# The weights of 32 experts, regrouped by the host: one row of 16 KB or 8 KB for each partition in place of rows of 2 KB and 4 KB

## The chip, the core and the metric

The kernel runs on one core of one Trainium2 chip. The metric is the device time of one execution in microseconds. Before the change three runs took 2957.39 to 2959.16 us, with a median of 2958.98 us.

## What the kernel computes

All of it is one launch in 32-bit floats, on 512 tokens of 1024 channels. A first block (rmsnorm, sparse attention beside a linear recurrence, a dense feed-forward, a gated embedding) takes the first half of the time and is not touched by the change. A second block has two layers. Each modulates its input by a vector, mixes tokens by windowed attention and local mixers, projects by `w_out`, normalizes, and then passes the tokens through a hierarchical mixture of experts. Layer 0 sends 768 tokens there (512 and 256 of a context), layer 1 only the 512. Cut to what matters here:

```python
# hier_moe(h, ...): h is [n, 1024]; 4 groups of 8 experts, top 1 group, top 2 experts in it
g_val, g_idx = lax.top_k(hf @ w_rg + b_rg, 1)
e_val, e_idx = lax.top_k(e_logit_of_the_group, 2)
gates  = p_group[:, None] * jax.nn.softmax(e_val, axis=-1)
expert = g_idx * 8 + e_idx
...
# for each block of tokens that go to one expert e; w1, w3: [32, 1024, 512], w2: [32, 512, 1024]
y = (jax.nn.silu(xb @ w1[e]) * (xb @ w3[e])) @ w2[e]
...
return jnp.zeros_like(h).at[slot_tok].add(ys * slot_gate[:, None])
```

An expert's weights are 2.10 MB for each of w1, w3 and w2. With 32 experts a layer's weights are 201 MB, and on-chip memory holds those of three experts at a time.

## The kernel before

The expert stage of a layer is the function `experts(l)` (L1788 to L1953). Its tokens have been sorted by expert into *items* of 64 slots in layer 0 and of 32 slots in layer 1; each item belongs to one expert. The static part of the program handles 41 items in layer 0 and 51 in layer 1, and a loop at its end takes what may be left over. Which expert an item has is known only at run time: SP, the engine that issues the weight loads, reads the number `eid` and a flag `new` from memory into registers.

For one item the work is this. POOL gathers the tokens' rows with an indirect DMA (L1813), some items ahead. PE transposes them (L1819, ACT copies them out at L1821), then multiplies by w1 and w3 in two halves (`first`, L1832; the result is the tile `ph`). `silu` is a tanh on ACT (L1838) and two steps on DVE (L1839, L1840). PE transposes again, then multiplies by w2 in two halves (`second`, L1847, tile `py`). `scatter` scales the result by the gate on DVE (L1859; in layer 0 a step at L1858 first prepares the tile `ys`), and POOL writes it to DRAM with an indirect DMA (L1860). The tile `ys` has three buffers in layer 0, and L1858 is the first to write one again. The program's order on PE is fixed by hand: an item's second product runs behind the first product of the next item.

**Places for weights.** There are three. Each holds two tiles of 16 KB per partition for w1 and w3 (`R13`, shape 128 x 4 x 2 x 512: in each of four row blocks the row of w1, then that of w3) and two tiles of 8 KB per partition for w2 (`R2`, 128 x 2 x 1024). Even items use place 0, odd items places 1 and 2 by turns:

```python
def place(i):
    return 0 if i % 2 == 0 else 1 + i // 2 % 2
...
ld(i + (4 if i % 2 else 2), n)     # behind each product group n of item i
```

`ld(i, n)` (L1881 to L1888) asks for piece n of item i: pieces 0 and 1 are halves of w1 and w3, 2 and 3 halves of w2. It is called behind the product group that used that piece of the place last, so two items ahead for even items and four ahead for odd ones. The load carries the condition `new > 0`: where the place already holds that expert, the DMA is skipped, but its instruction remains. Even items run through the experts with the most items, so long runs of them load nothing; odd items mostly take a new expert each.

**The load itself** is `expert_load` (L1770 to L1786). Pieces 0 and 1 are two DMAs of 1 MB each, one from w1 and one from w3, whose rows are 512 floats or 2 KB. Pieces 2 and 3 are one DMA of 1 MB each with rows of 1024 floats or 4 KB. An item has six loads. In the trace they are all written `r<-w`, on SP's queue, L1786, or L1782 for those without a condition.

**What else is on the queue.** Three experts are chosen ahead, and their weights are loaded without a condition before the routing is known: `load_front` (L1726) for place 0, `open_second` and `open_third` for place 1, `open_fourth` and `expert_store` for place 2. Around them `wload` (L159 to L165) loads other weights in rows of 1 KB, among them the chunks of `w_out`, that ACT (L156) and DVE (L157) split into two parts for PE. At the end `moe_norm` (L1959) reads the tile `yd` back in rows of 8 KB. SP issues one DMA after the other; each has one of eight completion semaphores, DMAHW0 to DMAHW7 by turns, and an instruction that reuses one waits until the DMA that had it before has landed. What the text doesn't pin in order (`pin`) is placed by the scheduler of the framework that builds the program.

Of the kernel before, what the change touches and what calls it, by code (L numbers as in the profile page):

```python
# [32 lines left out]
def constants():  # L33
    c = {}
# [19 lines left out]
    # for the routing: 0.., order of experts, 8.., 256 (token tile - 128), offsets of the parts of rows, 2 p, p;  # L54
    # the work block of an item: a + total * b - places of the second lane * c
# [14 lines left out]
class Stream:  # L70
    """Column chunks of weights [1024, 256 each], split into (hi, lo) by halves of their rows, a half
    ahead of the products; the last ones are only loaded. The chunks asked for count from a base."""
# [33 lines left out]
class Kern:  # L106
# [16 lines left out]
    def rsqrt(self, pool, v, scale, eps):  # L123
        """1/sqrt(v*scale+eps) for a [128, 1] tile: a bit guess and three Newton steps, each on a
        multiple c of the root (c becomes -2 c^3), divided out in the end."""
# [21 lines left out]
    def mm3(self, out, stat, mov, start, stop):  # L147
        """out += stat.T @ mov with each side a (hi, lo) pair."""
        nc = self.nc
        (sh, sl), (mh, ml) = stat, mov  # L150
        nc.tensor.matmul(out, sh, mh, start=start, stop=False)  # L151
        nc.tensor.matmul(out, sh, ml, start=False, stop=False)  # L152
        nc.tensor.matmul(out, sl, mh, start=False, stop=stop)  # L153
# [13 lines left out]
    def wchunk(self, ap, kt, cols, pool=None, raw=None):  # L167
        """A [kt*128, cols] piece of a weight as a list of kt (hi, lo) pairs [128, cols]."""
# [68 lines left out]
    def vectors(self, z, engine):  # L237
        """Per-channel vectors with the channel on the partition."""
# [15 lines left out]
    def norm_hT(self, pool, x, gain, hi, lo, work):  # L254
        """rmsnorm of x [128, 4, 1024] (token, channel), transposed to (hi, lo) [128, 8, 512]."""
# [39 lines left out]
    def proj(self, w, N=512):  # L295
        """The two 128-channel tiles of a 256-column chunk as [channel, token] in PSUM."""
# [10 lines left out]
    def projg(self, W, c, N):  # L307
        """The same from a stream, in steps."""
# [12 lines left out]
    def fill(self):  # L321
        """One step of work that is not tied to the place where it runs."""
        if self.bg is not None:
            next(self.bg, None)
# [11 lines left out]
    def mixer(self):  # L336
        nc, tc, a = self.nc, self.tc, self.a
        with ExitStack() as st:
# [21 lines left out]
            # gates: 0.5 * sigmoid, [token, tile, 48]  # L360
# [45 lines left out]
    def keys(self, m):  # L406
        """Keys of groups 2m, 2m+1 with (hi, hi) and (lo, lo) stacked."""
# [16 lines left out]
    def compress(self, kp):  # L424
        """Compressed keys (hi, hi / lo, lo stacked) and values (two copies of the 32 rows)."""
# [57 lines left out]
    def gelu2(self, out, x, pool, shape, tag):  # L483
        """2 * gelu(x) (tanh form); x in SBUF."""
# [7 lines left out]
    def pair(self, t, Q, KD):  # L492
        """Heads 2t and 2t+1: half the gated sum of the three branches, [channel, token]."""
# [4 lines left out]
        # compressed branch  # L498
# [34 lines left out]
        # the two dense branches  # L533
# [43 lines left out]
    def rnn_vectors(self):  # L577
# [11 lines left out]
        # softplus(-lam) = max(-lam, 0) + log1p(exp(-|lam|)), exp as ((1+t)/(1-t))^16 with t = tanh(-|lam|/32)  # L589
# [9 lines left out]
        # log1p(e) = 2 atanh(z), z = e / (2 + e) <= 1/3  # L599
# [21 lines left out]
    def rnn(self, c, yA):  # L621
        """Channels 256c..: conv, RG-LRU and the mixing gates; the sum with yA to y (hi, lo)."""
# [22 lines left out]
        for m in range(2):  # L645
# [9 lines left out]
            # y = (1 + exp(log_a)) / 2 is about 1/(1-th), th = tanh(log_a / 2), and one Newton step makes it so  # L655
# [5 lines left out]
            # a = (1+th)/(1-th), sqrt(1-a^2) = 2 sqrt(-th)/(1-th)  # L661
# [23 lines left out]
    def row(self, pool, name, ap, n=D, engine=None):  # L685
        """A vector on all partitions."""
        t = pool.tile([128, n], F32, name=self.nm(name), tag=name)
        (engine or self.nc.scalar).dma_start(t, bass.AP(tensor=ap.tensor, offset=ap.offset, ap=[[0, 128], [1, n]]))
        return t

    def mix_out(self, xb):
        """x + rmsnorm(y @ w_out)."""
# [17 lines left out]
    def norm_add(self, x, o, g, pool):  # L710
        """x += rmsnorm(o) * g for one token tile."""
# [66 lines left out]
    def ple(self):  # L778
        """x + sigmoid(x @ w_gate + b) * (p @ w_proj), by [channel, token]; leaves x and its transpose."""
# [48 lines left out]
    def modulation(self, pool, pp, pt_pool):  # L828
        """silu(c) @ w_ada + b_ada for both conditionings, a step at a time: by rows in DRAM
        (modd) and by channel on the partition (modT)."""  # L830
# [58 lines left out]
    def mcol(self, l, r, n):  # L889
        """Modulation vector n of layer l and conditioning r, channel on the partition: [128, 8]."""  # L890
        return self.modT[l][:, r, 8 * n:8 * n + 8]

    def mrow(self, pool, l, r, n, tag, engine=None):
        """The same on all partitions: [128, 1024]."""
# [11 lines left out]
    def transposeN(self, src, n, j, tag="pp"):  # L906
        """Channel tile j of n token tiles, transposed into PSUM: [128, n * 128]."""
# [5 lines left out]
    def affine_split(self, hi, lo, src, sc, sh, pool):  # L913
        """(hi, lo) of src * sc + sh with per-partition scalars."""
# [81 lines left out]
    def open_route(self, l, NT, pool, kv):  # L996
        """What the routing keeps of each token tile, and the routers' biases."""
# [14 lines left out]
    def logit_parts(self, l, r, wg, c12):  # L1012
        """For the logits of (t scale + shift) gs + bs, which are scale (t @ wg) + shift c1 + c2."""
# [24 lines left out]
    def open_side(self, l, r):  # L1038
        """Tokens of the sequence (r = 0) or of the context (r = 1)."""
# [15 lines left out]
    def side_input(self, c):  # L1055
        """The modulated input, transposed, as (hi, lo); in the second layer with stops after the norms."""
# [40 lines left out]
    def stream(self, l):  # L1097
        """The chunks of w_in_2 and w_out_2 in the order of their use."""
# [3 lines left out]
    def tokpairs(self, W, c, NT):  # L1102
        """[token, 256] products, two token tiles to a PSUM bank."""
# [8 lines left out]
    def rope(self, out, src, i, nh, wk):  # L1112
        """Axial rotary embedding of token tile i: src [128, nh * 64] in PSUM."""
# [12 lines left out]
    def project(self, c):  # L1126
        """Keys, values and queries, attention and the local mixers: c.mix."""
# [82 lines left out]
    def attention(self, Q, NT, r, mix, wk, sp, op_):  # L1210
        """All heads: window and context keys (sequence) or context keys only. The scores run ahead of
        the transposes of the weights."""
# [5 lines left out]
        for u in range(len(units) + LAG):  # L1218
# [10 lines left out]
            if nl:  # L1229
# [3 lines left out]
                # key block m, queries of block n at slot n - m + 1  # L1233
# [27 lines left out]
    def scores(self, h, n, q, NT, r, wk, sp):  # L1261
        """The softmax of one head and query block: [query, window keys and context keys]."""
# [87 lines left out]
    def layer_norm(self, x, src, pool):  # L1350
        """x = (src - mean) / sqrt(var + eps) over the channels of one token tile."""
# [7 lines left out]
    def ln_scale(self, st, pool):  # L1359
        """(scale, shift) that normalize a token tile."""  # L1360
# [8 lines left out]
    def side_out(self, c, po, steps=None):  # L1369
        """o @ w_out, first layer norm, the expert input (to DRAM) and the router's logits, whose  # L1370
        products run behind; steps: of other work, to go between."""
# [71 lines left out]
        def logits(t, h, w):  # L1443
            """Of half the channels of a token tile, in two steps."""
# [73 lines left out]
    def pick(self, i0, i1, le, pool):  # L1518
        """The group and, in each group, the first and second expert of token tiles i0 .. i1 as one-hot
        rows; the first of equals is taken."""  # L1520
# [42 lines left out]
    def route(self, l, NT, ep):  # L1563
        """Experts, gates and the list of work: blocks of slots, each of one expert. The experts are
        ordered by their number of blocks; the first and the last are given."""
# [13 lines left out]
        with ExitStack() as st:  # L1579
# [13 lines left out]
            # blocks of the experts, [all, expert] and on the partition, and where they begin  # L1593
# [22 lines left out]
            # slots  # L1616
# [9 lines left out]
            # the place of work block d, u = total - 1 - d: 2 d, or else, of each two odd places the first for  # L1626
            # 0 <= u <= nb and the second for others; u = 1 has place 3
# [8 lines left out]
            # rows of a slot, in ng parts: ng times its token, less an offset where it is in use, and the choice  # L1636
# [19 lines left out]
            # items: expert of each, and how many  # L1656
# [19 lines left out]
            # odd items have two places  # L1676
# [6 lines left out]
            # gates  # L1683
# [29 lines left out]
    def given(self, s):  # L1713
        """The expert whose weights are in place s before the routing."""
        return slice(STATIC[s], STATIC[s] + 1)

    def open_front(self, l):
        """Places for the weights of the experts: some are there before the routing, for experts that are
        given their items."""
# [20 lines left out]
    def place16(self, name, *shape, dt=F32):  # L1740
        """One of four places of 16 KB: for a chunk of w_out, then for an expert's weights."""
# [28 lines left out]
    def expert_load(self, l, s, n, e, cond=None, engine=None, pin=None):  # L1770
        """Pieces 0, 1: half the rows of w1 and w3; 2, 3: half the rows of w2; to place s."""
        nc, a = self.nc, self.a
        pick = lambda w, r: a[w][l][e, r, :]
        if n < 2:
            r = slice(n * 512, (n + 1) * 512)
            prs = [(self.R13[s][n][:, :, z, :], pick(w, r)) for z, w in enumerate(("w1_2", "w3_2"))]
        else:
            prs = [(self.R2[s][n - 2], pick("w2_2", slice((n - 2) * 256, (n - 1) * 256)))]
        for dst, src in prs:
            src = src.rearrange("o (k p) c -> p (o k) c", p=128)  # L1780
            if cond is None:
                d = (engine or nc.sync).dma_start(dst, src)  # L1782
                if pin:
                    pin(d)
            else:
                nc.sync.dma_start(dst, src, cond=cond, bounds_check="skip_entire_dma")  # L1786

    def experts(self, l, NT, ep):  # L1788
        """Items of some slots, one expert each. Even items take the experts from the front of the list,
# [211 lines left out]
```

## Time and profile before

| | |
|---|---|
| time, median of three runs | 2958.98 us |
| span of the profiled execution | 2959.7 us |
| PE (matmul) busy | 2529.7 us, 85% |
| DVE, ACT, POOL busy | 1376.6 us (47%), 864.8 us (29%), 446.9 us (15%) |
| bytes moved by DMA | 595.76 MB, mean 201 GB/s |
| of these on SP's queue q1 | 553.08 MB in 319040 packets, 51.7% of 16 engines |
| loads `r<-w` issued on SP | 580 of 1024 KB |

The table is of the whole span, and the stages differ a great deal: the expert stage of layer 0 lies at about 1592 to 2105 us, that of layer 1 at about 2464 to 2912 us. PE is the TensorE matmul, PEld its weight load, DVE VectorE, ACT ScalarE, POOL GpSimd, SP SyncE. SPq is SP's sequencer, which issues the DMAs of q1; POOL's gathers and scatters are on q0. A wait is written "waiting line <- what released it". The granted clock is TensorE's, 1.00 being full speed. A DMA share of 1.00 means that all 16 DMA engines of the core were busy. Times are of one profiled execution.

### The profile page before, as it was taken

How to read it: one execution, taken by the hardware profiler on the slowest of the kernel's cores; microseconds unless marked ns; L12 is line 12 of the kernel's file. 1: busy time of each engine (PE TensorE's matmuls, PEld its weight loads, DVE VectorE, ACT ScalarE, POOL GpSimd, SP SyncE). 2: the span in 40 equal slices, each digit the busy share in tenths (PEclk: the TensorE clock that was granted, in tenths of full speed). 3: DMA queues.
4: the chain of work that ended last, by engine and by line, in shares of the span. 5: the costliest groups of instructions: out<-in, count | busy, mean ns of one | idle time of the engine just before them, and what ended most of it. 6: DMA issues, size and time to landing. Idle time of an engine off the chain costs nothing. (4 is left out here: it accounts for less than half of the span.)

```text
span 2959.7 us, 45451 instructions
## 1 busy us (share of the span) xinstructions
PE 2529.7 (85%) x17077; PEld 1696.9 (57%) x17077; DVE 1376.6 (47%) x3629; ACT 864.8 (29%) x1765; POOL 446.9 (15%) x370
## 2 busy tenths in 40 slices
PE   7899999989999979878996999998468986667773
PEld 5767767777776867777783333332157773334441
DVE  4387787653332254777765212111468763111114
ACT  2265665532221123544421111100145421011111
POOL 0010010000100000030022321111130025322212
PEclk9899999999998989889997999999779997988997
DMA  3311212337776222341157999999611167999994
GB/s 119 101 43 61 63 34 72 108 115 227 233 238 213 93 86 77 101 153 44 43 215 279 377 392 410 410 407 408 253 45 58 36 255 277 362 393 370 355 355 172
DMA packets 348716, 595.76 MB, mean 201 GB/s; under 512 B 26948, under 2 KB 180104, under 8 KB 347216
## 3 DMA queue, kind: packets, MB, share of 16 engines
q1 hardware_dynamic: 319040, 553.08, 51.7%
q0 software_dynamic: 14400, 25.59, 2.4%
q10 hardware_dynamic: 15056, 14.17, 1.6%
q8 instruction: 137, 2.24, 0.3%
q14 instruction: 83, 0.68, 0.1%
HBM read 832.37 MB, written 25.92 MB: 290 GB/s over the span
## 5 line engine op out<-in xcount | busy, mean ns | idle before, releaser
L1832 PE MATMUL ph<-r,xT 128*32 128x256 f32 (+1 forms) x4576 | 513.0, 459 | 53.8 <-DMA r<-w 50.9
L157 DVE TENSOR_TENSOR wl<-wr,wh 128x1024 fp32r<-128x1024 f32 (+1 forms) x193 | 236.6, 1230 | 315.5 <-ACT wh L156 313.1
L1832 PEld LDWEIGHTS ph<-r,xT 128*32 128x32 f32 (+1 forms) x4576 | 201.8, 122 | 305.4 <-issue 233.4
L156 ACT ACTIVATE wh<-wr 128x1024 fp32r<-128x1024 f32 (+1 forms) x193 | 202.8, 1055 | 430.4 <-PE pj L152 213.9
L1847 PE MATMUL py<-r,aT 128*32 128x256 f32 (+1 forms) x2288 | 266.5, 475 | 67.7 <-DMA r<-w 67.7
L1847 PEld LDWEIGHTS py<-r,aT 128*32 128x32 f32 (+1 forms) x2288 | 99.6, 124 | 189.4 <-issue 145.3
L1821 ACT ACTIVATE aT<-tps 128x128 f32<-128x128 f32 (+1 forms) x92 | 29.8, 324 | 585.2 <-PE tps L1819 585.2
L1839 DVE SCALAR_TENSOR_TENSOR et<-et,ph 128x128 f32<-128x128 f32 (+1 forms) x92 | 31.8, 346 | 288.8 <-ACT et L1838 288.6
L1813 POOL DMA_INDIRECT xg<-hxd,tok x92 | 96.2, 1046 | 412.0 <-PE tps L1819 380.5
L151 PE MATMUL pj<-hh,wh 128*128 128x512 f32 x384 | 155.6, 406 | 1.7 <-ACT wh L156 1.7
L152 PE MATMUL pj<-hl,wh 128*128 128x512 f32 x384 | 154.0, 401 | 0.0
L153 PE MATMUL pj<-hh,wl 128*128 128x512 f32 x384 | 153.1, 400 | 0.0
L151 PE MATMUL tk<-wh,lh 128*128 128x256 f32 x416 | 130.4, 313 | 19.4 <-DVE k2l L1168 8.0
L1860 POOL DMA_INDIRECT yd<-ys,dst x92 | 93.2, 1013 | 344.0 <-DVE ys L1859 324.6
L1858 DVE SCALAR_TENSOR_TENSOR ys<-g2s,isc,g2s 128x512 f32<-128x512 f32 x41 | 30.6, 751 | 244.3 <-DMA yd<-ys,dst 244.3
L151 PE MATMUL pj<-h2h,wh 128*128 128x512 f32 x352 | 143.5, 408 | 0.1
L153 PE MATMUL pj<-h2h,wl 128*128 128x512 f32 x352 | 139.4, 396 | 0.0
L152 PE MATMUL pj<-h2l,wh 128*128 128x512 f32 x352 | 139.2, 396 | 0.0
L153 PE MATMUL tk<-wh,ll 128*128 128x256 f32 x416 | 127.0, 305 | 2.1 <-DVE ll L157 2.1
L152 PE MATMUL tk<-wl,lh 128*128 128x256 f32 x416 | 127.3, 306 | 0.0
L540 POOL TENSOR_SCALAR B<-dm 128x512 f32<-128x512 f32 x32 | 52.7, 1647 | 451.3 <-DVE z L555 258.2
L1405 POOL TENSOR_SCALAR s2r<-s2r 128x1024 f32<-128x1024 f32 x3 | 8.3, 2775 | 666.9 <-DMA s2r<-modd 666.9
(525 smaller groups left out, 5494.8 us busy)
## 6 DMA issues: line engine op xcount, KB each, us to landing
r<-w SPq DMA_DIRECT2D x580, 1024.0 KB
wr<-w_in SPq DMA_DIRECT2D x48, 1024.0 KB
adw<-w_ada SPq DMA_DIRECT2D x96, 512.0 KB
wr<-ffn_w_gate_up SPq DMA_DIRECT2D x22, 1024.0 KB
wr<-w_out SPq DMA_DIRECT2D x16, 1024.0 KB
wr<-ffn_w_down SPq DMA_DIRECT2D x10, 1024.0 KB
fy<-yd SPq DMA_DIRECT2D x10, 1024.0 KB
wr<-ple_w_gate SPq DMA_DIRECT2D x4, 1024.0 KB
```

Of the source, the lines that this page charges most:

```text
L151: nc.tensor.matmul(out, sh, mh, start=start, stop=False)
L152: nc.tensor.matmul(out, sh, ml, start=False, stop=False)
L153: nc.tensor.matmul(out, sl, mh, start=False, stop=stop)
L156: self.nc.scalar.activation(hi, src, AF.Copy)
L157: self.nc.vector.tensor_tensor(lo, src, hi.bitcast(F32), op=OP.subtract)
L540: nc.gpsimd.tensor_scalar(B, dm, SLOPE[h], None, op0=OP.mult)
L1813: pin(nc.gpsimd.indirect_dma_start(xg[i % XG], None, hx, bass.IndirectOffsetOnAxis(tokc.bitcast(U32), 0), bounds_check=NT * 128 * ng - 1, ...
L1832: pin(nc.tensor.matmul(H[group(g)], X[:, k % nx, group(k // nx)], R13[s][n][:, q, :, cs], start=k == 0, stop=k == 7, skip_group_check=True))
L1839: nc.vector.scalar_tensor_tensor(t, t, 1.0, H[:, 0:m], op0=OP.add, op1=OP.mult)
L1847: pin(nc.tensor.matmul(Y[group(g)], A[:, k % na, group(k // na)], R2[s][n][:, q, g * CX:(g + 1) * CX], start=k == 0, stop=k == 3, skip_gro ...
L1858: nc.vector.scalar_tensor_tensor(g, g2[1], isc, g2[0], op0=OP.mult, op1=OP.add)
L1860: d = nc.gpsimd.indirect_dma_start(yd, bass.IndirectOffsetOnAxis(dstc.bitcast(U32), 0), ys, None, bounds_check=NT * 256 * ng - 1, oob_is_e ...
```

## The change

The host stacks w1 and w3 and reorders all three weights before the launch. `w13_2` is [2, 32, 2, 128, 4096]: layer, expert, half, partition, and then the 4096 floats that this partition gets, in the order in which the tile `R13` holds them. `w2_2` is [2, 32, 2, 128, 2048] in the same manner. `expert_load` then moves a half of w1 and w3 as one DMA of 2 MB with one row of 16 KB for each partition, and a half of w2 as one DMA of 1 MB with one row of 8 KB for each partition. An item has four loads in place of six. The bytes, the places, the tiles, the calls and the conditions are as before.

```diff
     def expert_load(self, l, s, n, e, cond=None, engine=None, pin=None):
...
         nc, a = self.nc, self.a
-        pick = lambda w, r: a[w][l][e, r, :]
         if n < 2:
-            r = slice(n * 512, (n + 1) * 512)
-            prs = [(self.R13[s][n][:, :, z, :], pick(w, r)) for z, w in enumerate(("w1_2", "w3_2"))]
+            dst, src = self.R13[s][n].rearrange("p q z c -> p (q z c)"), a["w13_2"][l][e, n]
         else:
-            prs = [(self.R2[s][n - 2], pick("w2_2", slice((n - 2) * 256, (n - 1) * 256)))]
-        for dst, src in prs:
-            src = src.rearrange("o (k p) c -> p (o k) c", p=128)
-            if cond is None:
-                d = (engine or nc.sync).dma_start(dst, src)
-                if pin:
-                    pin(d)
-            else:
-                nc.sync.dma_start(dst, src, cond=cond, bounds_check="skip_entire_dma")
+            dst, src = self.R2[s][n - 2].rearrange("p q c -> p (q c)"), a["w2_2"][l][e, n - 2]
+        src = src.rearrange("o p f -> p (o f)")
+        if cond is None:
+            d = (engine or nc.sync).dma_start(dst, src)
+            if pin:
+                pin(d)
+        else:
+            nc.sync.dma_start(dst, src, cond=cond, bounds_check="skip_entire_dma")
...
+def expert_layout(w1, w3, w2):
+    w13 = np.stack([w1, w3], 3).reshape(2, 32, 2, 4, 128, 2, 512).transpose(0, 1, 2, 4, 3, 5, 6)
+    w2 = np.asarray(w2).reshape(2, 32, 2, 2, 128, 1024).transpose(0, 1, 2, 4, 3, 5)
+    return np.ascontiguousarray(w13).reshape(2, 32, 2, 128, 4096), np.ascontiguousarray(w2).reshape(2, 32, 2, 128, 2048)
...
 def kernel(**inputs):
...
+    arrays["w13_2"], arrays["w2_2"] = expert_layout(arrays.pop("w1_2"), arrays.pop("w3_2"), arrays["w2_2"])
```

The rest of the change blanks out comments. The lines behind L1772 are three lower in the changed kernel: L1786 becomes L1783, L1782 becomes L1779. SP's order has 1806 rows before and 1428 now. The order on PE and on POOL is the same.

The first place is SP in layer 1's expert stage. Before, one item's six loads and the first of the next item's stand so; `r_...` is a tile of a place, `w_2` any of the three weights, the numbers behind DMAHW are how far a semaphore has to have counted, and PE_49 is a count of PE:

```order
L1786 DMA r_19534<-w_2 128x4x512 [waits DMAHW1_49,PE_49]
...
L1786 DMA r_19534<-w_2 128x4x512 [waits DMAHW2_49]
...
L1786 DMA r_19535<-w_2 128x4x512 [waits DMAHW3_49,PE_49]
...
L1786 DMA r_19535<-w_2 128x4x512 [waits DMAHW4_49]
...
L1786 DMA r_3295_20142<-w_2 128x2x1024 [waits DMAHW5_49,PE_49]
...
L1786 DMA r_3295_20142<-w_2 128x2x1024 [waits DMAHW6_49,PE_49]
...
L1786 DMA r_3296_20169<-w_2 128x4x512 [waits DMAHW7_49,PE_49]
```

Between them stand the ISA rows of the condition and the reads of `eid` and `new`. In the changed kernel two whole items, the first with place 2 and the second with place 0, and the first load of a third stand on the same eight semaphores:

```order
L1783 DMA r_3259_19756<-w_2 128x4096 [waits DMAHW3_49,PE_49]
...
L1783 DMA r_3260_19757<-w_2 128x4096 [waits DMAHW4_49,PE_49]
...
L1783 DMA r_19494<-w_2 128x2048 [waits DMAHW5_49,PE_49]
...
L1783 DMA r_19495<-w_2 128x2048 [waits DMAHW6_49,PE_49]
...
L1783 DMA r_19444<-w_2 128x4096 [waits DMAHW7_49,PE_49]
...
L1783 DMA r_19445<-w_2 128x4096 [waits DMAHW0_49,PE_49]
...
L1783 DMA r_3295_20048<-w_2 128x2048 [waits DMAHW1_49,PE_49]
...
L1783 DMA r_3295_20048<-w_2 128x2048 [waits DMAHW2_49,PE_49]
...
L1783 DMA r_3296_20075<-w_2 128x4096 [waits DMAHW3_49,PE_49]
```

DMAHW3 comes round again after eight loads: before, that is one item and two loads of the next; now it is two items.

The second place is SP at the head of layer 0's stage, where the weights of place 0 are loaded ahead beside two chunks of `w_out`. Before:

```order
L1782 DMA r_12824<-w_2 128x4x512
L161 DMA wr_12841<-w_out 128x8x256
L161 DMA wr_12848<-w_out 128x8x256
L1782 DMA r_12824<-w_2 128x4x512
L1782 DMA r_12825<-w_2 128x4x512 x2
L1782 DMA r_12875<-w_2 128x2x1024
L1782 DMA r_12876<-w_2 128x2x1024
```

Now:

```order
L1779 DMA r_12824<-w_2 128x4096
L161 DMA wr_12841<-w_out 128x8x256
L161 DMA wr_12848<-w_out 128x8x256
L1779 DMA r_12825<-w_2 128x4096
L1779 DMA r_12875<-w_2 128x2048
L1779 DMA r_12876<-w_2 128x2048
```

Ahead of the two chunks stood one load of 1 MB, and now stands one of 2 MB; layer 1's stage has the same.

The third place is DVE a little later, where the chunks of `w_out` (tile `wo`) are split. Before:

```order
L157 TENSOR_TENSOR wo_2319_12843<-wr_12841,wo_2319_12843 128x1024 x2
L157 TENSOR_TENSOR wo_2321_12850<-wr_12848,wo_2321_12850 128x1024 x2
L1424 TENSOR_TENSOR st_12943<-o_12945,g1r_12861 128x512
L1425 SCALAR_TENSOR_TENSOR st_12943<-x,st_12943 128x512
L1426 BN_STATS lst_12944<-st_12943 128x6
```

Now:

```order
L157 TENSOR_TENSOR wo_2319_12843<-wr_12841,wo_2319_12843 128x1024 x2
L1424 TENSOR_TENSOR st_12941<-o_12943,g1r_12861 128x512
L1425 SCALAR_TENSOR_TENSOR st_12941<-x,st_12941 128x512
L157 TENSOR_TENSOR wo_2321_12850<-wr_12848,wo_2321_12850 128x1024 x2
L1426 BN_STATS lst_12942<-st_12941 128x6
```

The split of the last chunk, `wo_2321`, stands behind the two sums of one token tile now; on ACT its other half (L156) moves behind one copy in the same way.

## Rows read from the trace of the kernel before

**Rows 1.** The page: rate in 40 slices of 74 us.

```profile
GB/s 119 101 43 61 63 34 72 108 115 227 233 238 213 93 86 77 101 153 44 43 215 279 377 392 410 410 407 408 253 45 58 36 255 277 362 393 370 355 355 172
```

**Rows 2.** ACT's timeline, layer 0: start, duration (us), instruction, [idle before <-releaser].

```profile
1617.66 0.38 ACT L1838 ACTIVATE et<-ph 128x256 f32<-128x256 f32 x1 [3.21 <-PE ph L1832]
1629.22 0.38 ACT L1838 ACTIVATE et<-ph 128x256 f32<-128x256 f32 x1 [3.21 <-PE ph L1832]
...
2096.98 0.38 ACT L1838 ACTIVATE et<-ph 128x256 f32<-128x256 f32 x1 [3.15 <-PE ph L1832]
```

**Rows 3.** Waits of PE, 1590 to 2110: us in total, times, longest.

```profile
PE py L1847 <- DMA r<-w: 12.9, 7, 3.5
PE ph L1832 <- DMA r<-w: 6.1, 2, 3.9
```

**Rows 4.** Length; busy us (count): PE, PEld, DVE, ACT, POOL; clock, DMA share, GB/s.

```profile
1872.00:2087.00 215.00, 195.88 (x874) 66.34 (x875) 38.32 (x71) 22.73 (x50) 30.11 (x29) 0.96 1.04 406
2500.00:2880.00 380.00, 280.30 (x4103) 148.72 (x4096) 43.88 (x124) 38.42 (x123) 95.20 (x86) 0.89 0.99 372
```

**Rows 5.** Waits of PE, 2495 to 2915.

```profile
PE py L1847 <- DMA r<-w: 54.8, 19, 10.5
PE ph L1832 <- DMA r<-w: 44.8, 20, 14.8
```

**Rows 6.** DMA from 2700 to 2730: rate in 40 slices of 0.75 us.

```profile
GB/s 380 399 410 401 407 254 380 385 418 377 407 407 252 134 339 431 421 339 404 399 366 142 347 385 380 361 404 355 401 404 418 407 404 412 407 421 317 199 423 404
```

**Rows 7.** Waits of SP's queue, 2495 to 2915.

```profile
SPq L1786 <- DMA r<-w: 139.4, 67, 4.0
```

**Rows 8.** Waits of SP's queue, 1590 to 2110.

```profile
SPq L1786 <- PE tps L1819: 61.1, 32, 4.3
```

**Rows 9.** DMA from 1519 to 1523, rows of 2 KB alone.

```profile
DMA packets 787, 1.56 MB, mean 391 GB/s; under 512 B 31, under 2 KB 31, under 8 KB 786
```

**Rows 10.** DMA from 1525 to 1528, rows of 4 KB alone.

```profile
DMA packets 331, 1.28 MB, mean 425 GB/s; under 512 B 16, under 2 KB 16, under 8 KB 331
```

**Rows 11.** DMA from 2921 to 2928, rows of 8 KB alone.

```profile
DMA packets 413, 2.99 MB, mean 427 GB/s; under 512 B 48, under 2 KB 48, under 8 KB 48
```

**Rows 12.** Queues, 1872 to 2087: packets, MB, share of 16 engines.

```profile
q1 hardware_dynamic: 34660, 82.55, 97.8%
q0 software_dynamic: 2320, 4.57, 5.5%
```

**Rows 13.** Queues, 2500 to 2880.

```profile
q1 hardware_dynamic: 56278, 134.05, 94.1%
q0 software_dynamic: 3840, 6.53, 4.8%
```

**Rows 14.** Timeline of SP's queue at the head of layer 1's stage.

```profile
2373.26 0.38 SPq L1782 DMA_DIRECT2D r<-w  x1
2379.38 6.99 SPq L161 DMA_DIRECT2D wr<-w_out  x2
```

**Rows 15.** Timeline of one item, layer 0: POOL, DVE, PE's weight load.

```profile
1854.03 1.01 POOL L1860 DMA_INDIRECT yd<-ys,dst  x1 [3.36 <-DVE ys L1859]
...
1860.15 0.75 DVE L1858 SCALAR_TENSOR_TENSOR ys<-g2s,isc,g2s 128x512 f32<-128x512 f32 x1 [6.40 <-DMA yd<-ys,dst]
...
1861.27 0.42 DVE L1840 SCALAR_TENSOR_TENSOR et<-et,ph 128x256 f32<-128x256 f32 x1
...
1867.87 0.20 PEld L1819 LDWEIGHTS tps<-ident,et 128*128 128x128 f32 x2 [0.81 <-issue]
```

**Rows 16.** Queues, 1853 to 1863.

```profile
q1 hardware_dynamic: 1459, 3.71, 93.2%
q0 software_dynamic: 160, 0.42, 10.6%
```

**Rows 17.** Queues, 1772 to 1781.

```profile
q1 hardware_dynamic: 956, 3.53, 95.7%
```

**Rows 18.** Timeline of DVE at 1779.

```profile
1779.13 0.75 DVE L1858 SCALAR_TENSOR_TENSOR ys<-g2s,isc,g2s 128x512 f32<-128x512 f32 x1 [6.29 <-DMA yd<-ys,dst]
```

## The prediction

> **What bounds the kernel now.** I read the page first, slice by slice [rows 1]. Two stretches move 350 to 410 GB/s, slices 23 to 28 and 33 to 39: the expert stages of layers 0 and 1. Everywhere else the DMA engines have room, so faster weight transfers can be worth something only there. Next the stretches by engine and the waits of PE.
>
> In layer 0 (41 items) the products of an item take 11.56 us when nothing is late: the tanh at L1838 comes at 1617.66 and 1629.22, and 39 items later than the first of these at 2096.98 [rows 2]. Without stalls that would be 39 x 11.56 = 450.8 us; it is 479.3, so 28.5 us are lost. 19.0 us of it PE stands waiting for weights, 12.9 + 6.1 [rows 3]; the rest I put down to the slower granted clock around the stalls (0.96 in the stretch that holds them) [rows 4]. All of them come after 1872. From there to 2087 the DMA engines move 406 GB/s without a pause, share 1.04 [rows 4].
>
> In layer 1 (51 items of half the columns) PE waits 54.8 + 44.8 = 99.6 us for weights [rows 5], and is busy for only 280 of 380 us [rows 4]. That stage is bound by the loads. But there the engines move only 372 GB/s, and in close view the rate drops again and again, to 254, 134, 142 and 199 GB/s for a slice of 0.75 us [rows 6]: the queue runs dry for moments although PE is starving. The waits of SP, which issues the loads, say why: 139.4 us in this stage for earlier loads to land [rows 7]. The order shows the mechanism: SP's loads take turns on eight completion semaphores, DMAHW0 to 7, so no more than eight loads, skipped ones counted, are under way; the ninth waits for the first. An item takes six of the eight, so SP looks one item and a third ahead, and most even items load nothing. In layer 0 SP waits instead for PE to give a place free, 61.1 us for one product group alone [rows 8], and the queue does not run dry.
>
> **Rows of 16 and 8 KB.** Stretches with one row length alone: rows of 2 KB (w1, w3) 391 GB/s, rows of 4 KB (w2) 425, rows of 8 KB (the read of yd at the end) 427 [rows 9 to 11]. Rows of 16 KB are not in the trace. From 2 to 4 KB there is a gain of 34 GB/s, from 4 to 8 of 2, so I take 427 for 16 KB too. An expert is 4.19 MB of w1 and w3 and 2.10 MB of w2: 10.73 + 4.93 = 15.66 us before, 9.82 + 4.91 = 14.73 after, so 0.93 us less. The ends: 0, if long rows are cut into short ones on their way, and 0.97 if 16 KB gives 2 GB/s more again.
>
> These prices account for the stages. Layer 0 from 1872 on: 82.55 MB on SP's queue is 13.1 experts, 205 us, and the gathers and scatters on the other queue 5.5% of 215, 12 us [rows 12]: 217 against 215 measured, no dry time. Layer 1 from 2500 to 2880: 134.05 MB is 21.3 experts, 334 us, and 4.8% of 380, 18 us [rows 13]: 352 against 380. So 28 us of dry time.
>
> The Trainium skill speaks against this term: "DMA: Bandwidth & Descriptors", section "Where 436 GB/s comes from", says that for transfers between HBM and SBUF the HBM side binds, at about 358 GB/s for one core. Then rows could be as long as they like. The trace is above it for 215 us at 406 and disagrees; by that rule the term would be nil.
>
> The same page, section "Why small descriptors are slow (HBM only)", gives some 3 cycles per packet beside one cycle for 32 bytes: 67 cycles for 2 KB. By that alone the estimate is about 0.5 us for an expert and not 0.93, and the two terms below would be some 15 us smaller in all; the measured step from 391 to 427 is about twice as large, so the rows decide.
>
> **Layer 0: 15 us.** Up to 1872 PE never waits, and faster loads only end earlier and wait for a place: nothing. From there the queue is always full, so the 13.1 experts behind bring 13.1 x 0.93 = 12 us, and with the stalls some of the slow clock goes (28.5 us were lost for 19.0 of waiting). I take 15. The ends are 0 and 28.5, where PE has no stall left and is the bound.
>
> **Layer 1: 38 us.** The rates alone bring 21.3 x 0.93 = 20. The rest is the look-ahead. w1 and w3 in one transfer make four loads of an item instead of six, and the same eight semaphores now hold two whole items: at the moment when SP's next load is let go, the second half of w1 and w3 and both of w2 of the expert before are still to come, 4 MB or some 10 us of work, where it was one or two transfers of 1 MB. The dry time of 28 us should shrink. What may stay is at an item that changes the expert in the even place: its loads may start only when PE has given up the place. I count 18 of the 28, so 38; ends 0 and 48. PE, busy for 280 of 380 us with part of it at a lower clock, is no bound at 342.
>
> **What costs nothing or is hidden.** SP issues fewer instructions, 378 rows fewer in its order. At the head of each stage 2 MB instead of 1 now stand before two chunks of w_out on SP. The load is issued at 2373.26, the chunks only at 2379.38, since they wait for a buffer [rows 14]; 2.1 MB at 427 GB/s take 4.9 us of these 6.1. In layer 0 the same pause is longer. If that cover goes, 2.5 us per layer. The split of the last chunk moves behind one copy on ACT and behind two sums on DVE; PE needs that chunk only after nine other products, so 0.
>
> Sum: 15 + 38 = 53 off the profiled span of 2959.7 gives 2906.7; that span is 0.7 over the median of 2959.0, so 2906.
>
> **Rivals.**
> The dry spells stay (chance 0.20). For it: PE must free places first, and the longest waits are at changes of the even expert. Against: SP waits for landings 139 us and hardly for PE there. Then 15 + 20 = 35 go: 2924.
>
> No stall is left in layer 0 and no dry spell in layer 1 (0.12). For it: the mean price of layer 0 becomes 205 us where PE has 186.5 to do, so only a few stalls need to fall otherwise. 28.5 + 48 = 76: 2883.
>
> The ceiling (0.05): long rows are cut on the way or bring no more, and the depth does not matter. For it: 425 to 427 is flat. Against: two thirds of the bytes are now on the 391 side. The rule of 358 GB/s would end here. 0 to 5 us: 2956.
>
> Slower, through the scatter (0.08). In layer 0 the scatter of an item is issued at 1854.03, and DVE stands at L1858 until it has landed, 1860.15; behind it on DVE are the two steps of the next silu, the second starting at 1861.27 and ending at 1861.69. PE needs that at 1867.87: 6.2 us of slack [rows 15]. The scatter shares the 16 engines with the loads. 160 packets for a gather and a scatter in that stretch [rows 16] are 5 each per engine for the scatter; if each waits for one weight packet of 16 KB (614 ns at 427 GB/s over 16 engines) instead of one of 2 KB (84 ns at 391), the landing comes 5 x 0.53 = 2.7 us later, inside the slack. Against a steeper rise: where the packets are mostly of 4 KB [rows 17] DVE waits 6.29 us, with the mixed ones 6.40 [rows 15, 18]. It decides from a delay of 6.2 us on; at 9 us it would cost 2.8 x 38 items = 106, less the 38 of layer 1: 3027. Layer 1 has no L1858 and is spared.
>
> **How the numbers follow.** The forecast has 0.55. Faster by over 0.2% (5.9 us, about what a measurement of this kernel tells from no change): 0.55 + 0.20 + 0.12 = 0.87; within: 0.05; slower: 0.08. The range reaches from the best case to half-way between the dry-spell rival and no change: 2880 to 2944.
>
> **What would show it.** After: stretches of 16 KB rows at about 427 GB/s and the mean of layer 1 at 400 or more; no slices far below 380 between loads there; SP's wait for landings below 70 us; PE's wait for weights below 70 us in layer 1 and below 12 in layer 0; DVE's wait at L1858 below 10 us each and PE without waits for DVE. A 16 KB stretch below 400 GB/s, or PE waiting for the silu in layer 0, would make the prediction wrong.

## The result and the profile after

The changed kernel takes 2904.41 us, the median of four runs (2898.85 to 2906.55), against 2959.07 us before: a ratio of 0.9817, with a 95% interval of 0.9803 to 0.9831. That is 54.7 us less. The forecast was 2906, 53 less. The sum was right; its terms were not, and that the errors cancel is in part luck (below).

The profiled execution is the fastest of the four, with a span of 2897.0, and 62.7 us shorter than the profiled one of before. PE's order is the same in both, so its instructions can be matched one by one. 9.0 us of the lead are there at 320 us, long before the first expert, where the change does nothing. All seven later profiles lead the profile of before by 3.2 to 6.7 us at that point, also that of a kernel that loads its weights in the same rows and transfers as before (e4 below). So that part is chance, mostly a slow start of the one execution of before. The rest arises in the two expert stages, but for 1.7 us between them, no more than the runs differ there (376.2 to 379.5 us).

Layer 0 first: ACT's timeline, the tanh L1835 of the second and third item and of the last, as in [rows 2].

```profile
1609.83 0.38 ACT L1835 ACTIVATE et<-ph 128x256 f32<-128x256 f32 x1 [3.21 <-PE ph L1829]
1621.39 0.38 ACT L1835 ACTIVATE et<-ph 128x256 f32<-128x256 f32 x1 [3.21 <-PE ph L1829]
...
2077.40 0.38 ACT L1835 ACTIVATE et<-ph 128x256 f32<-128x256 f32 x1 [3.15 <-PE ph L1829]
```

An item still takes 11.56 us. From the first of these rows to the last, 39 items later, it is 467.6 us where [rows 2] have 479.3: 11.7 us are won. PE's waits in that stage, to compare with [rows 3]:

```profile
PE ph L1829 <- DMA r<-w: 8.1, 3, 3.7
PE py L1844 <- DMA r<-w: 4.6, 7, 1.4
```

They fell from 19.0 to 12.7 us; the granted clock of the stretch rose from 0.96 [rows 4] to 0.99. Next the two stretches of [rows 4], matched by PE's instructions, the second only roughly (length, busy us of PE, PEld, DVE, ACT and POOL, clock, DMA share, GB/s):

```profile
1864.00:2067.00 203.00, 189.57 (x874) 63.74 (x874) 36.17 (x64) 22.75 (x50) 30.31 (x29) 0.99 1.00 421
2478.00:2820.00 342.00, 276.43 (x4152) 142.24 (x4156) 44.46 (x126) 39.19 (x125) 96.12 (x86) 0.91 0.99 413
```

In layer 1 SP's queue moves the same 134 MB in 342 us instead of 380, and the mean rate is 413 GB/s instead of 372. PE's 4103 products of the second row of [rows 4] take 338.7 us now; the row here has 49 more. PE's waits for weights there fell from 99.6 us [rows 5] to 65.4. SP's own waits, in the third row, rose against [rows 7]:

```profile
PE ph L1829 <- DMA r<-w: 52.0, 19, 14.7
PE py L1844 <- DMA r<-w: 13.4, 4, 9.3
```

```profile
SPq L1783 <- DMA r<-w: 162.7, 58, 5.9
SPq L1783 <- PE py L1844: 28.4, 21, 7.0
```

Where [rows 6] dropped to 134 and 142 GB/s for a slice of 0.75 us, the same items now run without a gap. This is DMA from 2655 to 2685:

```profile
GB/s 437 415 502 371 410 421 377 431 421 442 426 426 398 373 415 459 416 448 404 426 459 459 371 404 437 393 393 431 453 437 426 350 434 407 440 418 404 459 448 459
DMA packets 1493, 12.68 MB, mean 423 GB/s; under 512 B 351, under 2 KB 355, under 8 KB 507
```

From 2500 to 2743 the rate looks like this throughout. Two gaps are left before the loads end. The first is from 2743 to 2751, in this window of 2735 to 2765. By SP's records the last load of item 37 is issued at 2734.9 and the next one that moves bytes, the first of item 38, at 2748.0; between them stand four that are skipped, of items 39 and 36, and two of these wait for semaphores:

```profile
GB/s 459 415 404 415 415 415 481 415 366 426 333 328 328 317 317 286 212 120 371 44 208 382 437 366 431 486 350 530 377 464 393 481 415 415 448 415 437 393 481 415
```

SP's waits from 2735 to 2760 are for landings, not for PE to give up the place:

```profile
SPq L1783 <- DMA r<-w: 10.4, 3, 4.8
SPq L1783 <- PE py L1844: 0.3, 1, 0.3
```

The second gap, from 2812 to 2818, is deeper. Eight skipped loads stand there before the first load of item 49, which is issued at 2815.9. But PE never waits for weights between 2795 and 2845, so this gap costs nothing. The window is 2795 to 2825:

```profile
GB/s 459 453 410 404 421 470 431 426 371 437 481 424 402 393 415 426 404 382 437 410 442 393 295 205 134 11 0 0 0 306 153 350 437 393 459 366 426 448 442 415
```

A stretch of 16 KB rows alone, 2555 to 2562, answers [rows 9 to 11]:

```profile
DMA packets 205, 3.01 MB, mean 431 GB/s; under 512 B 21, under 2 KB 21, under 8 KB 21
```

### The profile page after: what moved, and what is told of

It reads as the page before. It is cut to its first block, busy times and chain, and to the rows that moved or that the text cites. A ratio compares the mean times of both kernels' runs of the same rounds, so it can differ in the third digit from the quotient of the medians.

```text
span 2897.0 us, 44870 instructions
## 1 busy us (share of the span) xinstructions
PE 2509.1 (87%) x17077; PEld 1681.6 (58%) x17077; DVE 1382.8 (48%) x3629; ACT 864.8 (30%) x1765; POOL 445.7 (15%) x370
## 4 chain that ended last, share of the span: by engine, by line
PE 66%; DVE 14%; DMA 13%; ACT 3%; issue 2%; SPq 0%; ACTq 0%; POOL 0%; POOLq 0%; DVEq 0%
DMA r<-w 12%; PE ph L1829 11%; PE pj L151 7%; PE pj L152 7%; PE pj L153 7%; PE py L1844 5%; PE oT L571 2%; PE tk L151 2%; PE tps L1816 2%; PE tk L153 2%; PE ada L877 2%; PE tk L152 2%; PE dn L152 1%; PE dn L151 1%; PE dn L153 1%
## 5 line engine op out<-in xcount | busy, mean ns | idle before, releaser
L156 ACT ACTIVATE wh<-wr 128x1024 fp32r<-128x1024 f32 (+1 forms) x193 | 202.8, 1055 | 426.0 <-PE pj L152 214.1
L1844 PE MATMUL py<-r,aT 128*32 128x256 f32 (+1 forms) x2288 | 253.1, 452 | 18.8 <-DMA r<-w 18.0
L1855 DVE SCALAR_TENSOR_TENSOR ys<-g2s,isc,g2s 128x512 f32<-128x512 f32 x41 | 40.4, 989 | 301.5 <-DMA yd<-ys,dst 301.4
L1844 PEld LDWEIGHTS py<-r,aT 128*32 128x32 f32 (+1 forms) x2288 | 92.2, 119 | 135.7 <-issue 90.5
L153 PE MATMUL pj<-h2h,wl 128*128 128x512 f32 x352 | 139.4, 396 | 0.0
L540 POOL TENSOR_SCALAR B<-dm 128x512 f32<-128x512 f32 x32 | 52.2, 1631 | 445.2 <-DVE z L555 257.1
```

Of the source, the lines that this page charges most:

```text
L156: self.nc.scalar.activation(hi, src, AF.Copy)
L1844: pin(nc.tensor.matmul(Y[group(g)], A[:, k % na, group(k // na)], R2[s][n][:, q, g * CX:(g + 1) * CX], start=k == 0, stop=k == 3, skip_gro ...
```

## The experiments

Theory A is the prediction's: row length and look-ahead each have a share. Theory B gives all to the number of packets, nothing to the look-ahead. Theory C came up with the first results: not how far SP looks ahead, but the size of a transfer itself. The table has each median, its ratio to the runs of before on the same chip with the interval, and from its profile the time between the first and the last tanh of each layer (before: 1608.78 to 2096.98 and 2475.95 to 2907.47, so 488.2 and 431.5 us). Each kernel has one profile; that of e2 is the slowest of its four executions, 6.3 us over their median; the others lie within 3 us of theirs.

| run | loads an item | rows of w1 w3 / w2 | median us | ratio | layer 0 us | layer 1 us |
|---|---|---|---|---|---|---|
| e0, the change again | 4 | 16 / 8 KB | 2903.28 | 0.9824 (0.9811 to 0.9838) | 476.2 | 390.4 |
| e1 | 4 | 2 / 4 KB | 2926.39 | 0.9902 (0.9887 to 0.9917) | 488.6 | 404.0 |
| e2 | 6 | 8 / 8 KB | 2927.20 | 0.9899 (0.9883 to 0.9914) | 474.2 | 420.2 |
| e3 | 4 | 4 / 4 KB | 2915.52 | 0.9869 (0.9854 to 0.9884) | 482.6 | 396.9 |
| e4 | 6, none skipped | 2 / 4 KB | 2922.57 | 0.9881 (0.9863 to 0.9899) | 489.0 | 399.3 |
| e5 | 4, none skipped | 16 / 8 KB | 2897.27 | 0.9801 (0.9786 to 0.9817) | 476.4 | 386.6 |
| e6 | 4 and 3 | 16 / 8 and 16 KB | 2902.85 | 0.9817 (0.9801 to 0.9833) | 476.7 | 390.5 |

The kernel before had a median of 2955.46 beside e0 to e3, and of 2956.69 beside e4 to e6.

**e0, the change once more.** Expected: 

> The changed kernel once more, as the measure for the three others. In its profile 8 to 9 us of the lead over the kernel before arose in the first 320 us, where the change touches nothing, and the profiled run was the fastest of four (2898.85, the others 2903 to 2907). If that early lead is chance, the median is 2904 to 2906 again and a new profile has less of it; if it belongs to the change, every profile has 8 us there and the median of the stages alone would be 46.

The median is 2903.28, 52.2 under before, and this profile's early lead is 4.8 us, not 9.0. The stages repeat to 0.3 us: 476.2 and 390.4 against 476.4 and 390.1 in the first profile of the change. So the part of the change is what the stages show, 12.0 and 41.1 us.

**e1, four loads with short rows.** The host lays a piece out so that one transfer carries w1 and w3, but in rows of 2 KB.

```diff
-            dst, src = self.R13[s][n].rearrange("p q z c -> p (q z c)"), a["w13_2"][l][e, n]
+            prs = [(self.R13[s][n].rearrange("p q z c -> p (q z) c"),
+                    a["w13_2"][l][e, n].rearrange("o b p c -> p (o b) c"))]
...
+            src = a["w2_2"][l][e, (n - 2) * 256:(n - 1) * 256, :].rearrange("o (k p) c -> p (o k) c", p=128)
+            prs = [(self.R2[s][n - 2], src)]
```

Expected: 

> Four loads an item as in the changed kernel, but the host lays the pieces out so that rows stay 2 KB (w1, w3) and 4 KB (w2). Theory A, that of the prediction (row length 35 us, look-ahead 18): only the look-ahead is left, 2959 - 18 = 2941. Theory B (time goes by the number of packets alone, the look-ahead is worth nothing): no change, 2956 to 2962.

29.1 us are won, more than A's 18 and far from B's 0. All of it is in layer 1 (27.5 us); layer 0 is as before (-0.4). B has fallen: half of the gain needs no longer row at all.

**e2, six loads with long rows.** The changed layout, but a half of w1 and w3 as two transfers of 1 MB, each the half of every row.

```diff
-            dst, src = self.R13[s][n].rearrange("p q z c -> p (q z c)"), a["w13_2"][l][e, n]
+            dst = self.R13[s][n].rearrange("p q z c -> p (q z c)")
+            src = a["w13_2"][l][e, n].rearrange("o p f -> p (o f)")
+            prs = [(dst[:, h * 2048:(h + 1) * 2048], src[:, h * 2048:(h + 1) * 2048]) for h in range(2)]
```

Expected: 

> Rows of 8 KB for all three weights, but six loads an item: a half of w1 and w3 is two transfers of 1 MB again. Theory A: only the rows are left, 2959 - 35 = 2924, and the rate in layer 1 drops between loads as before. Theory B: nearly the whole gain, 2904 to 2910.

28.3 us are won: A had 35, B nearly all of the 52, and neither came. In layer 0 it is 14.0, as much as the whole change brings there; in layer 1 only 11.3. The drops are still there, now between long rows, here 208 and 295 GB/s (DMA from 2670 to 2700, slices of 0.75 us); the 30 us from 2650 on have slices of 142 and 137:

```profile
GB/s 208 404 404 427 371 426 415 306 382 404 339 355 432 459 393 448 393 448 415 393 426 415 295 393 404 382 346 404 415 361 360 415 371 366 388 393 437 371 404 415
DMA packets 1828, 11.69 MB, mean 390 GB/s; under 512 B 344, under 2 KB 344, under 8 KB 456
```

Its mean rate over layer 1's stretch is 379 GB/s, hardly above the 372 of before, while in layer 0 it has 422 (length, busy by engine, clock, share, GB/s):

```profile
1880.00:2040.00 160.00, 153.04 (x710) 50.72 (x706) 30.42 (x54) 18.76 (x41) 26.97 (x25) 1.00 1.01 422
2483.00:2854.00 371.00, 289.67 (x4140) 147.55 (x4136) 44.23 (x126) 39.07 (x125) 96.07 (x86) 0.88 0.96 379
```

So the two parts are two effects in two places: longer rows in both layers, fewer loads in layer 1 alone. Apart they win 27.5 + 11.3 = 38.8 us in layer 1, together 41.1.

**e3, four loads, all rows of 4 KB.** w1 and w3 stand side by side in DRAM, with no further regrouping.

```diff
-    w13 = np.stack([w1, w3], 3).reshape(2, 32, 2, 4, 128, 2, 512).transpose(0, 1, 2, 4, 3, 5, 6)
...
+    w13 = np.concatenate([w1, w3], 3)
```

Expected: 

> Four loads an item; w1 and w3 stand side by side in DRAM, so that a row is 4 KB, and w2 is as before, also 4 KB. Theory A (425 GB/s at 4 KB against 427, 0.07 us an expert, some 34 experts): 2.4 us over the changed kernel, 2907. Theory B (single packets take 159 ns at 4 KB, 309 at 8 KB and 611 at 16 KB in the traces, so an expert 15.27 us against 14.72): half of the gain, about 2930. Between them: 0.55 x 34 = 19 us over the changed kernel, if the packets' own times decide and the look-ahead is worth what A says.

It is 12.2 us slower than the changed kernel, so rows above 4 KB are worth something, and A's price of 2.4 us was wrong; B's 2930 was wrong the other way. The next two stretches show why: with the queue full, rows of 4 KB alone move at 421 GB/s in this run (2564 to 2574) and rows of 8 KB alone at 427 in e2 (2597 to 2606).

```profile
DMA packets 1060, 4.21 MB, mean 421 GB/s; under 512 B 33, under 2 KB 33, under 8 KB 1060
```

```profile
DMA packets 524, 3.84 MB, mean 427 GB/s; under 512 B 55, under 2 KB 55, under 8 KB 55
```

By these rates, and 431 for 16 KB, rows of 4 KB throughout cost 0.30 us an expert over the changed kernel, 10 us for 34 experts. The third expectation, 19 us from the packets' own times, was too much. With short rows an engine's packets overlap in time: the DMA share in e1's full stretch of layer 0 is 1.04 at 408 GB/s, in the changed kernel's 1.00 to 1.01 at 421 to 426.

**e4, the kernel before without its skipped loads.** The items that load a new expert are known for these inputs, so the others' loads are left out of the program. What moves, in which rows and transfers, is as before; this kernel serves these inputs only.

```diff
-                if i >= NS:
+                if i >= NS or i not in NEED[l]:
                     return
```

Expected: 

> The kernel before, with its six loads and its rows, but the loads that are skipped at run time for these inputs are not in the program, so that each of the eight semaphores carries a load that moves bytes. What is moved, in which rows and in which transfers, is as before. Theory A (SP may look only eight loads ahead, and skipped ones use up the look-ahead): layer 1 wins 25 to 28 us as with four loads an item, 2955 - 27 = 2928. Theory C (transfers of 2 MB are better than two of 1 MB by themselves, because each load begins with a slow packet on every engine): the loads are as many and as small as before, no change, 2952 to 2958.

34.1 us are won, more than A's 25 to 28; by the profile 32.2 us are won in layer 1 and nothing in layer 0 (-0.8). C has fallen: the transfers are the old ones of 1 MB. What changed is how many bytes eight semaphores cover, and how much SP itself has to do. SP no longer waits for a weight load to land in layer 1; its waits, 2488 to 2876, are mostly for PE's places now, where [rows 7] had 139.4 us for landings:

```profile
SPq L1786 <- PE tps L1819: 58.6, 29, 9.7
SPq L1786 <- PE py L1847: 41.4, 19, 6.0
SPq L1931 <- DMA yd<-ys,dst: 24.3, 2, 18.1
SPq L1786 <- PE ph L1832: 7.5, 4, 4.7
```

One rival is left. A load that is left out, or merged with another, saves SP its own time too: by the issue records about 0.47 us for each skipped load, and 135 of the 269 loads that SP reaches between 2476 and 2880 in the kernel before are skipped, some 64 us of its time as an estimate. e1 and e4 shorten that and free semaphores at once, so they do not tell how the gain divides between the two. The stage's rate is 402 GB/s with the old rows:

```profile
2492.00:2843.00 351.00, 278.49 (x4149) 144.22 (x4146) 44.51 (x126) 39.48 (x126) 96.10 (x86) 0.89 1.03 402
```

**e5, the changed kernel without its skipped loads.** The same edit on the changed kernel. Expected: 

> The changed kernel without its skipped loads. Theory A: the look-ahead of two items leaves some 11 us in layer 1 (6.5 to 7 us of idle engine time, 4.4 of slow packets); part of that goes, 2895 to 2901. Theory C: no change from the changed kernel, 2903. Against the run without skipped loads of the kernel before, the rows alone should be worth the 25 us that rows were worth with six loads (14 in layer 0, 12 in layer 1) by both.

The median is 2897.27, and layer 1 takes 386.6 us, 3.8 less than in e0. The expected 2895 to 2901 came, but the intervals of the two ratios overlap, so from the times alone the gain is not certain. Against e4 the rows are worth 25.3 us, as expected (12.6 in layer 0, 12.7 in layer 1). So by one profile each, the skipped loads cost about 4 us with the change where they cost 32 before. The gap at item 38 is gone in this run (the lowest slice from 2730 to 2760 is 339 GB/s).

**e6, w2 as one transfer in places 1 and 2.**

```diff
+            src, h = a["w2_2"][l][e], slice((n - 2) * 2048, (n - 1) * 2048)
+            if s == 0:
+                dst, src = self.R2[0][n - 2].rearrange("p q c -> p (q c)"), src[:, :, h]
+            elif n == 2:
+                return
+            else:
+                dst = self.R2w[s - 1].rearrange("p h q c -> p (h q c)")
```

Expected: 

> The changed kernel with w2 as one transfer of 2 MB and one row of 16 KB for each partition in places 1 and 2 (place 0 keeps two halves), so an odd item has three loads. Theory A: the look-ahead grows from 2 to 2.3 items, and a row of 16 KB takes 611 ns where two of 8 KB take 618, some 0.06 us an expert: together 2 to 5 us less, 2898 to 2901, if PE does not lose what it gains because the first half of w2 comes 2.4 us later. If that decides, in layer 0 some 2 us at each of its late items are added: 2905 to 2912.

No difference: 0.9817 against 0.9817 and 0.9824 of the changed kernel, and the stages agree to 0.5 us. The 2 to 5 us less did not come, nor the loss. Neither the further look-ahead nor the later first half can be measured. No run here that serves any input is faster than the change beyond what the runs differ.

## Why the prediction came out right, step by step

**The bound.** Right. Nothing outside the two expert stages moved with the change, and the time between the stages is 377.3 us against 379.0, where the other runs have 376.2 to 379.5.

**The price of the rows: mis-sized.** 0.93 us an expert came from a 2 KB stretch of 391 GB/s [rows 9] and a 4 KB stretch of 425 [rows 10]. Both are 3 to 4 us long and stand ahead of the stages, and neither holds in them. In the kernel before, from 2591 to 2600, where the queue is full, rows of 2 KB alone move at 408:

```profile
DMA packets 1843, 3.67 MB, mean 408 GB/s; under 512 B 49, under 2 KB 49, under 8 KB 1843
```

With 408 and 421 for before, 431 and 427 for after, an expert takes 4.19/0.408 + 2.10/0.421 = 15.26 us before and 4.19/0.431 + 2.10/0.427 = 14.64 after: 0.62 us, two thirds of the forecast. The stretch of layer 0 agrees: its 87.3 MB take 7.7 us less at 421 than at 406 GB/s, 0.59 us for each of 13.1 experts. The Trainium skill's page "DMA: Bandwidth & Descriptors", section "Why small descriptors are slow (HBM only)", had led to an estimate of some 0.5 us, which I set aside for the two short stretches. Here it was closer than my rows. The 358 GB/s of the Trainium skill's section "Where 436 GB/s comes from" on the same page did not bind this kernel on its one core: it moved 421 GB/s over 203 us, 80.7 of 85.4 MB of it on SP's queue of loads.

**Layer 0: 15 forecast, 11.7 to 12.0 measured.** 13.1 experts by 0.62 are 8.1 us, and not the 12 of the forecast. The rest comes from a term that the prediction put at nothing, the loads up to 1872. That "faster loads only end earlier and wait for a place" does not hold: at the head of the stretch, at the same product of PE, the changed kernel has moved 2.0 MB more on SP's queue, and the stretch itself moves 80.7 MB there where [rows 12] have 82.6. At 421 GB/s that is some 4 us. PE sees the gain from the other side, as 6.3 us less waiting and 6.3 us less busy time for the same 874 products (195.88 to 189.57) at the higher clock, which was argued and came. e1 and e4 show that nothing of it is look-ahead (-0.4 and -0.8), e2 that rows alone do it (14.0).

**Layer 1, rows: 20 forecast, 11.3 to 13.6 measured** (alone in e2, on top of four loads from e1 to e0). 21.3 by 0.62 is 13.2.

**Layer 1, look-ahead: 18 of 28 forecast, 27.5 measured** in e1. The dry time goes with fewer loads, and e4 shows it by taking away only the skipped loads; that it is the semaphores' doing and not SP's own time is shown in part (see e4). The size was wrong, and for the same reason as the rows: with rows that seem too slow, the queue's work explains too much of the stage, and too little is left as dry time. The 28 us of dry time came from 334 us for the weights. At 15.26 us an expert they are 325, and with the 18 us of the other queue 343 of 380 are accounted for: 37 are left. Of these 27.5 went with four loads and 32.2 with no skipped ones. Rows 9 and 10 moved about 8 us from one term to the other, and the sum did not notice. The forecast was some 3 us too high in layer 0, 7 too high for layer 1's rows and 9.5 too low for the look-ahead. Part of that balance follows from one wrong price in two terms; that the rest came out even is luck, since 18 of 28 had no row behind it.

**What costs nothing.** Right. At the head of layer 1's stage (SP's timeline) the load is issued at 2352.10 and the chunks of `w_out` at 2360.21, a pause of 8.1 us for the 4.9 us of the load, where [rows 14] had 6.1:

```profile
2352.10 0.33 SPq L1779 DMA_DIRECT2D r<-w  x1
2360.21 4.82 SPq L161 DMA_DIRECT2D wr<-w_out  x2
```

**The slower rival.** Its mechanism is there, inside the slack. DVE's wait for the scatter (us in total, times, longest), before at L1858 and after at L1855:

```profile
DVE ys L1858 <- DMA yd<-ys,dst: 244.3, 38, 7.5
DVE ys L1855 <- DMA yd<-ys,dst: 301.4, 38, 10.2
```

DVE waits 1.5 us longer on the mean (7.9 against 6.4), where 2.7 had been worked out, and the longest wait is 2.7 longer. The slack was 6.2 [rows 15], and PE waits for the silu in layer 0 for 1.5 us, once, as before. Where it would turn was not tried.

**What was to show it.** Three signs came as written: 16 KB rows at 431, a mean of 413 in layer 1, PE's wait there at 65.4. The slices far below 380 are gone but for the two gaps at items 38 and 49. The prediction had left room for a gap at item 38, but for another reason, that PE gives up the even place late; SP's waits there are for landings, with skipped loads holding semaphores. Two were just missed: 12.7 for 12 in layer 0, and single scatter waits over 10. One was a bad sign: SP's wait for landings should have fallen below 70 and rose to 162.7. SP also waits for landings when eight transfers of a full queue are ahead of it. The wait says that SP stands at a semaphore, not that the queue is dry; in e4 it is gone, in e5 39.6 us are left. Only the rate in close view tells the two apart. The upper end of the range, 2944, is not half-way between the dry-spell rival and no change, which is 2941.5; nothing hangs on it.

## What to carry to other kernels

Take the price of a transfer from a long stretch in which the queue is full, not from the first microseconds of a load; an error in it moves between "work" and "dry time", and a right sum can hide it. Where transfers share a fixed number of completion semaphores, count how many bytes these cover, and count skipped transfers too: here fewer loads in the old rows brought 27.5 of 41 us in layer 1. To tell the size of a transfer from their number, leave out the transfers that move nothing and keep the rest; that also shortens the issuing engine's own work, which this does not separate. And look whether faster loads get ahead before the stretch in which they are waited for.

## What the runs showed of the hardware

Single packets on SP's queue take 84, 159, 309 and 611 ns for 2, 4, 8 and 16 KB (medians of the packet records, before and after). That is about 8 ns a packet and 27 bytes a nanosecond. In rows of 2 KB alone (before, 2591 to 2600) the packets' times add up to 105.0% of the time of 16 engines, in rows of 16 KB alone (after, 2555 to 2562) to 100.6%: short packets overlap, and at 408 GB/s one of 2 KB costs an engine 80 ns.

With six loads an item some packets are slow. In e2's layer 1 (2483 to 2854) about 800 of 16270 packets of 8 KB, in groups of up to some 20, take 0.4 to 1.9 us each. Summed over the stretch of layer 1 (2500 to 2880 before) as time of 16 engines, packets lose 19.3 us against their medians in the kernel before and 20.7 in e2, both with six loads; 4.7 in e1, 4.4 in e4 and 4.6 in the changed kernel. What makes them slow is not shown. It is not simply an empty queue: 43 of the 78 groups of three or more in e2 (starts within 0.3 us of one another) have 15 or 16 packets under way throughout the microsecond before. A DMA share near 1 hides them, since a slow packet counts as busy: the stretch with 0.99 in [rows 4] is the one whose rate drops to 134 GB/s in [rows 6].
